# A fourth tile for raw weights, loads one unit earlier, and two sums of the last gate and up columns made by accumulating DMAs: a float32 decoder block on one Trainium2 core

## The chip, the cores and the metric

One Trainium2 chip, of which the program uses one core. The metric is the device time of one execution in microseconds (us): the median of three runs, and beside it one execution that the hardware profiler recorded.

## What is computed

The reference is one decoder block in float32 on x of 512 tokens by 2048 channels. Cut to what matters here:

```python
h = modulate(rms_norm(x, g_mix), sh1, sc1)        # the mixing half: w_in, two attentions, w_out
...
h = modulate(rms_norm(x, g_ffn), sh2, sc2)        # the feed-forward half
a = causal_dwconv(h @ w_gate, conv_w, conv_b)     # w_gate: 2048 x 5632
y = (jax.nn.silu(a) * (h @ w_up)) @ w_down        # w_up: 2048 x 5632, w_down: 5632 x 2048
x = x + gt2 * y
return rms_norm(x, g_final)
```

The change concerns the way in which weights reach TensorE. Most of its lines are in helpers that every projection uses, and what it alters in the work of an engine other than the queues is in the feed-forward half: gate, up and down.

## The kernel before, in words

**Units.** Every projection is cut into units, each a block of a weight matrix of about 128 x 1024 to 128 x 1792 numbers. A unit passes through a pipeline: SP loads the raw block from HBM into a tile of pool `wraw` (3 tiles); ScalarE (ACT) copies it into a rounded high part `wh` (L226 or L230), VectorE (DVE) subtracts that from the raw block to make the low part `wl` (L227 or L231), both in pool `wsp` (3 tiles each); TensorE (PE) then makes three products per pair of factors (high by high, high by low, low by high: L334 to L336 in `mm3`).

**Seven products.** The gate, up, down, w_out and most of the w_in gate columns use a Strassen-Winograd scheme: seven products of half blocks in place of eight, each of them three matmuls. A unit holds two sets of seven, so it is 2 x 7 x 3 = 42 matmuls with 256 moving columns. The weight side needs seven blocks b0 to b6, of which four are raw quarters of the weight block and three are sums. They are made in two ways:

- kind "seven" (gate, up, w_out, w_in gates; `US`): SP loads the four quarters with two DMAs (L183); DVE makes the first two sums in one instruction (L212) and the two that follow from them in two more (L213, L214).
- kind "right" (down; `UR`): SP loads one quarter twice into the places of the first two sums (L191), then the other three (L192, L193); GpSimd (POOL) issues two accumulating DMAs that add a second quarter to each from HBM (L195), after the loads have landed. DVE makes only L213 and L214.

**The look-ahead.** `ahead()` runs before each unit's products are emitted, and keeps three units converted. When it converts unit n it first emits the loads up to unit n + 2 (with L195, where the unit has it), then the copy and subtraction of unit n, then the sums of unit n + 1. With three raw tiles the load of unit n + 2 writes into the tile of unit n - 1, so SP waits there until L227 of unit n - 1 has ended; what stands behind it on SP waits too. Every engine executes in the order in which the program emits; nothing is reordered.

**The order of the feed-forward half.** 44 columns of gate and up with four units each (`proj_seven`, 22 pairs), with `combine` (L448 to L455), the convolution (L1437 to L1444) and the gating (L1459) of earlier columns in between; the gated result goes to HBM in tiles `g` (L1463). Then the down projection in three chunks of 8, 8 and 6 steps: for each chunk, columns of 512 outputs (4, 4 and 3 of them), each of 8, 8 or 6 units, 82 units in all. The left factors of a chunk are made from `g` (loads L1600, sums L1610 to L1613, parts L1627 to L1633) during the last gate/up column, the last column of the chunk before or the first column of the chunk. At the end of a column ACT copies the eight PSUM banks out (`leave`, L467), DVE combines (L473 to L479), and the result is stored by SP (L1672, first chunk) or added to the stored one by POOL (L1674, second chunk). The last 512 outputs of the last chunk are six plain units (L201, L230, L231).

All other intermediate data lives in `slots`, a pool of 65 tiles of 128 x 512. `first_ada`, in the first 200 us, loads the columns of w_ada ahead into such slots (L292).

Of the kernel before, what the change touches and what calls it, by code (L numbers as in the profile page):

```python
# [37 lines left out]
NSLOT = 65  # L38
# [52 lines left out]
OF2 = 1  # L91

# [12 lines left out]
def block_kernel(ctx, tc, x, c, w_ada, b_ada, g_mix, w_in, w_o_sb, w_o_dsa, w_out, rel_bias,  # L105
# [12 lines left out]
    wraw = pool("wraw", 3)  # L118
# [19 lines left out]
    units, raws, summed_, parts, at = [], [], [], [], [0]  # L138
# [5 lines left out]
    def US(w, k0, c0, fn):  # L144
        steps.append(((w, k0, 4, c0, 256, "seven"), fn))
        units.append(steps[-1][0])

    def UR(w, k0, c0, fn):
        steps.append(((w, k0, 2, c0, 512, "right"), fn))
        units.append(steps[-1][0])  # L150
# [21 lines left out]
    def seven_blocks(r, kind):  # L172

        q = 2 if kind == "seven" else 1
        return r.rearrange("p (q b c) -> p q b c", q=q, b=8)

    def load(spec):
        w, k0, nk, c0, nn, kind = spec
        raw = wraw.tile([128, 2048], F32, tag="raw", name="raw")
        if kind == "seven":  # L180
            for i in range(2):
                k = 128 * (k0 + 2 * i)
                nc.sync.dma_start(raw[:, 1024 * i + 512:1024 * (i + 1)].rearrange("p (k n) -> p k n", n=nn),  # L183
                                  w[k:k + 256, c0:c0 + nn].rearrange("(k p) n -> p k n", p=128))
            return raw
        if kind == "right":

            b = seven_blocks(raw, kind)[:, 0]
            wb = w[128 * k0:128 * (k0 + 2), c0:c0 + nn].rearrange("(k p) (u c) -> p k u c", p=128, u=2)
            for u in range(2):  # L190
                nc.sync.dma_start(b[:, 2 + u], wb[:, 1, 1])  # L191
            nc.sync.dma_start(b[:, 4:6], wb[:, 0])  # L192
            nc.sync.dma_start(b[:, 6], wb[:, 1, 0])  # L193
            for u in range(2):
                nc.gpsimd.dma_start(b[:, 2 + u], wb[:, u, 1 - u], accum_op=OP.add)  # L195
            return raw
# [7 lines left out]

    def sums_of(r, spec):

        kind = spec[5]
        if kind not in ("seven", "right"):
            return
        b = seven_blocks(r, kind)  # L210
        if kind == "seven":
            nc.vector.tensor_add(b[:, :, 2:4], b[:, :, 5:7], b[:, :, 7:8].to_broadcast([128, 2, 2, 128]))  # L212
# [3 lines left out]
    def convert(r, spec):  # L216
# [4 lines left out]
        if kind in ("seven", "right"):  # L221
            b = seven_blocks(r, kind)
# [1256 lines left out]
    for i in range(2):  # L1479
        proj_seven([ffn[-2 + i][0]], h2)  # L1480
# [303 lines left out]
```

## Time and profile before

| what | value |
|---|---|
| median of three runs | 3045.23 us (3038.62 to 3046.95) |
| the profiled execution, its own time | 3040.32 us |
| its span | 3038.6 us |
| mean granted TensorE clock | 0.972 |
| HBM read / written | 453.10 MB / 51.92 MB |

The span is the time from the first to the last recorded instruction; 1.7 us lie around it. The rows of the trace are read as follows. In a table of windows, each row gives a stretch of the span, then the busy time of each engine with the number of its instructions, the granted TensorE clock, the mean busy share of the 16 DMA engines and what they moved. In a list of waits, "A line <- B line: total, times, longest" says how long an engine stood still before an instruction, and whose end let it go. In a timeline, a row has start, duration, engine, line, what is written and read, and in brackets the idle time before it with what ended that.

### The profile page before, as it was taken

The page shows a single profiled execution, that of the slowest core. Times are in us where ns is not written, and L with a number is a line of the kernel's source. Part 1 is how long each engine was busy: PE and PEld are TensorE (multiplying, and loading weights), DVE is VectorE, ACT ScalarE, POOL GpSimd, SP SyncE. Part 2 cuts the span into 40 slices and gives each one's busy share as a digit, 9 for nine tenths or more (in the row PEclk, how much of TensorE's full clock was granted, in tenths as well). Part 3 has the DMA queues.
Part 4 walks back from the last instruction along what each step waited for, and adds up shares of the span by engine and source line. Part 5 has one row for each costly group of instructions (what it writes and reads, how often), then busy time and mean ns, then how long its engine had stood idle before and what let it go on. Part 6 is the DMA issues. An engine that isn't in the chain of part 4 may idle for free.

```text
span 3038.6 us, 52325 instructions
## 1 busy us (share of the span) xinstructions
PE 2890.5 (95%) x20287; PEld 2717.8 (89%) x20287; DVE 2496.0 (82%) x3677; ACT 1272.7 (42%) x1580; POOL 345.7 (11%) x372
## 2 busy tenths in 40 slices
PE   6899999999999999999988999999999999989887
PEld 5778889888888999888988999999999989989886
DVE  6877888888888887469989989988998997686778
ACT  4345433333344444224454444444444444353544
POOL 0000222201122000000122000000000013324330
PEclk8989999999999999999989999999999999989998
DMA  9664247777763445543452333333333357778996
GB/s 290 214 188 136 74 143 234 238 254 251 249 205 103 131 132 174 181 145 105 160 174 84 125 117 120 119 119 112 119 119 119 125 165 194 200 194 193 218 224 211
DMA packets 428520, 505.87 MB, mean 166 GB/s; under 512 B 34159, under 2 KB 328687, under 8 KB 428271
## 3 DMA queue, kind: packets, MB, share of 16 engines
q1 hardware_dynamic: 395439, 464.24, 48.2%
q0 software_dynamic: 25920, 25.70, 5.6%
q10 hardware_dynamic: 6912, 12.59, 1.1%
q8 instruction: 158, 2.59, 0.4%
q14 instruction: 91, 0.75, 0.1%
HBM read 453.10 MB, written 51.92 MB: 166 GB/s over the span
## 4 chain that ended last, share of the span: by engine, by line
PE 65%; DVE 15%; DMA 7%; issue 4%; ACT 2%; SPq 1%; POOL 0%; ACTq 0%; DVEq 0%; POOLq 0%
PE ps L334 21%; PE ps L336 21%; PE ps L335 21%; DMA raw<-in_w_down_dram 5%; DVE wl L227 4%; ACT wh L226 1%; DVE raw L213 1%; PE ps L957 1%; DVE slot L417 1%; DVE raw L212 1%; DVE slot L1633 1%; DVE raw L214 1%; DVE wl L231 0%; DMA slot<-x 0%; SPq L191 0%
## 5 line engine op out<-in xcount | busy, mean ns | idle before, releaser
L335 PE MATMUL ps<-slot,wh 128*128 128x256 f32 (+2 forms) x4624 | 1433.8, 310 | 18.8 <-DVE slot L412 16.4
L336 PE MATMUL ps<-slot,wl 128*128 128x256 f32 (+2 forms) x4624 | 1432.9, 310 | 10.4 <-DVE wl L227 10.4
L334 PE MATMUL ps<-slot,wh 128*128 128x256 f32 (+2 forms) x4624 | 1438.3, 311 | 4.1 <-ACT slot L411 2.4
L335 PEld LDWEIGHTS ps<-slot,wh 128*128 128x128 f32 (+1 forms) x4624 | 892.5, 193 | 63.4 <-DVE slot L412 18.0
L336 PEld LDWEIGHTS ps<-slot,wl 128*128 128x128 f32 (+1 forms) x4624 | 892.2, 193 | 57.1 <-DVE wl L227 12.6
L334 PEld LDWEIGHTS ps<-slot,wh 128*128 128x128 f32 (+1 forms) x4624 | 892.8, 193 | 50.8 <-ACT slot L751 4.5
L226 ACT CAST wh<-raw 128x1792 fp32r<-128x1792 f32 x338 | 571.2, 1695 | 716.5 <-DVE raw L214 404.8
L227 DVE TENSOR_TENSOR wl<-raw,wh 128x1792 fp32r<-128x1792 f32 x338 | 682.5, 2019 | 119.2 <-ACT wh L226 115.4
L334 PE MATMUL ps<-wh,slot 128*128 128x256 f32 (+1 forms) x1708 | 503.1, 295 | 35.0 <-ACT slot L467 29.8
L335 PE MATMUL ps<-wl,slot 128*128 128x256 f32 (+1 forms) x1708 | 500.8, 293 | 18.8 <-DVE wl L227 18.3
L336 PE MATMUL ps<-wh,slot 128*128 128x256 f32 (+1 forms) x1708 | 499.4, 292 | 4.8 <-DVE slot L514 4.8
L334 PEld LDWEIGHTS ps<-wh,slot 128*128 128x128 f32 x1708 | 338.0, 198 | 41.7 <-ACT slot L467 31.9
L335 PEld LDWEIGHTS ps<-wl,slot 128*128 128x128 f32 x1708 | 338.1, 198 | 24.0 <-DVE wl L227 21.0
L336 PEld LDWEIGHTS ps<-wh,slot 128*128 128x128 f32 x1708 | 338.0, 198 | 8.8 <-DVE slot L514 6.8
L231 DVE TENSOR_TENSOR wl<-raw,wh 128x1024 fp32r<-128x1024 f32 (+3 forms) x178 | 209.9, 1181 | 82.7 <-ACT wh L230 78.4
L195 POOL DMA_DIRECT2D raw<-in_w_down_dram x164 | 145.4, 1012 | 1154.5 <-DVE slot L1459 845.7
L230 ACT CAST wh<-raw 128x1024 fp32r<-128x1024 f32 (+3 forms) x178 | 177.5, 998 | 236.6 <-PE ps L335 172.5
L212 DVE TENSOR_TENSOR raw<-raw 128x512 f32<-128x512 f32 x256 | 178.2, 696 | 28.7 <-DMA raw<-in_w_up_dram 10.9
L213 DVE TENSOR_TENSOR raw<-raw 128x256 f32<-128x256 f32 x338 | 151.6, 449 | 56.2 <-DMA raw<-in_w_down_dram 47.3
L545 DVE SCALAR_TENSOR_TENSOR slot<-slot,c_act 128x512 f32<-128x512 f32 x240 | 192.0, 800 | 6.8
L214 DVE TENSOR_TENSOR raw<-raw 128x256 f32<-128x256 f32 x338 | 155.7, 461 | 11.6
L1266 POOL TENSOR_TENSOR mask<-mask,slot 128x512 f32<-128x512 f32 x13 | 19.0, 1458 | 553.5 <-ACT slot L1265 553.0
(224 smaller groups left out, 2241.6 us busy)
## 6 DMA issues: line engine op xcount, KB each, us to landing
slot<-in_w_ada_dram SPq DMA_DIRECT2D x368, 256.0 KB, 4.9
raw<-in_w_in_dram SPq DMA_DIRECT2D x118, 512.0 KB, 5.1
raw<-in_w_gate_dram SPq DMA_DIRECT2D x176, 256.0 KB, 3.1
raw<-in_w_up_dram SPq DMA_DIRECT2D x176, 256.0 KB, 3.1
raw<-in_w_down_dram SPq DMA_DIRECT2D x246, 128.0 KB, 4.2
raw<-in_w_in_dram SPq DMA_DIRECT2D x114, 256.0 KB, 2.9
raw<-in_w_down_dram SPq DMA_DIRECT2D x82, 256.0 KB, 4.7
raw<-in_w_down_dram POOLq DMA_DIRECT2D x164, 128.0 KB, 4.6
```

The source lines that it names most:

```text
L195: nc.gpsimd.dma_start(b[:, 2 + u], wb[:, u, 1 - u], accum_op=OP.add)
L212: nc.vector.tensor_add(b[:, :, 2:4], b[:, :, 5:7], b[:, :, 7:8].to_broadcast([128, 2, 2, 128]))
L213: nc.vector.tensor_add(b[:, :, 1], b[:, :, 3], b[:, :, 5])
L214: nc.vector.tensor_add(b[:, :, 0], b[:, :, 4], b[:, :, 1])
L226: nc.scalar.copy(hf, f)
L227: nc.vector.tensor_sub(l.rearrange("p (q f) -> p q f", q=n), f, hf.bitcast(F32))
L230: nc.scalar.copy(h, r)
L231: (nc.gpsimd if kind else nc.vector).tensor_sub(l, r, h.bitcast(F32))
L334: nc.tensor.matmul(o, lhsT=sh, rhs=mh, start=start, stop=False, skip_group_check=skip)
L335: nc.tensor.matmul(o, lhsT=sh, rhs=ml, start=False, stop=False, skip_group_check=skip)
L336: nc.tensor.matmul(o, lhsT=sl, rhs=mh, start=False, stop=stop, skip_group_check=skip)
L545: nc.vector.scalar_tensor_tensor(acc, raw[n], s, acc, op0=OP.mult, op1=OP.add)
```

## The change

- Pool `wraw` has 4 tiles, of 128 x 1792 in place of 128 x 2048; `slots` has 63 tiles in place of 65, and `first_ada` looks ahead `20 - len(hT)` in place of `22 - len(hT)` (never over 10).
- The seven blocks lie without a gap (7 blocks, not 8). In kind "seven" the quarter that is added to two others is loaded into the place of b0, so its load is three DMAs in place of two.
- `ahead()`, before the conversion of unit n, emits the loads up to unit n + 3, then the accumulating loads up to unit n + 2 (now a function of its own, `loaded_sums`), then the sums up to unit n + 1, and then the conversion of unit n.
- Kind "right" becomes "seven by dma", which also takes units of 4 x 128 rows by 256 columns. The gate and up columns from the 15th of the 19 pairs of the middle loop on, and those of the last two pairs, use it: 5 + 2 = 7 pairs by the code (the change's own words say eight), 14 columns, 56 units. Each loads five quarters with four DMAs on SP and adds two with two accumulating DMAs on POOL; DVE's L212 falls away there.

The diff, cut to its core:

```diff
-NSLOT = 65
+NSLOT = 63
+BY_DMA = 14
-    wraw = pool("wraw", 3)
+    wraw = pool("wraw", 4)
...
     def load(spec):
         w, k0, nk, c0, nn, kind = spec
-        raw = wraw.tile([128, 2048], F32, tag="raw", name="raw")
...
+        raw = wraw.tile([128, 1792], F32, tag="raw", name="raw")
+        if is_seven(spec):
+            b, wb = seven_blocks(raw, spec)
+            for u in (2, 3) if kind == "seven by dma" else (0,):
+                nc.sync.dma_start(b[:, :, u], wb[:, :, 1, 1])
+            nc.sync.dma_start(b[:, :, 4:6], wb[:, :, 0])
+            nc.sync.dma_start(b[:, :, 6], wb[:, :, 1, 0])
             return raw
...
+    def loaded_sums(r, spec):
+
+        if spec[5] == "seven by dma":
+            b, wb = seven_blocks(r, spec)
+            for u in range(2):
+                nc.gpsimd.dma_start(b[:, :, 2 + u], wb[:, :, u, 1 - u], accum_op=OP.add)
...
         while len(parts) < min(at[0] + 3, len(units)):
             n = len(parts)
-            loads(n + 3)
-            sums(n + 1 if units[n][5] == "right" else n + 2)
+            loads(n + 4)
+            while len(added_) < min(n + 3, len(units)):
+                loaded_sums(raws[len(added_)], units[len(added_)])
+                added_.append(True)
+            sums(n + 2)
             parts.append(convert(raws[n], units[n]))
             raws[n] = None
-            sums(n + 2)
...
-            first_load(n + min(AHEAD, 22 - len(hT)))
+            first_load(n + min(AHEAD, 20 - len(hT)))
...
     for n, (g, u) in enumerate(ffn[1:-2]):
-        proj_seven([g], h2)
-        proj_seven([u], h2)
+        proj_seven([g], h2, by_dma=n >= BY_DMA)
+        proj_seven([u], h2, by_dma=n >= BY_DMA)
...
-        proj_seven([ffn[-2 + i][0]], h2)
+        proj_seven([ffn[-2 + i][0]], h2, by_dma=True)
...
-    proj_seven([ffn[-2][1]], h2, left_start)
-    proj_seven([ffn[-1][1]], h2, h2_end)
+    proj_seven([ffn[-2][1]], h2, left_start, by_dma=True)
+    proj_seven([ffn[-1][1]], h2, h2_end, by_dma=True)
```

The order of the instructions on PE and ACT is the same in both kernels. It differs on DVE, SP and POOL. Lines of the changed kernel are shifted: its L190 to L192 are the loads that were L191 to L193 (and L183), its L207 the accumulating load L195, its L216 and L217 the sums L213 and L214, its L225 and L226 the copy and the subtraction that were L226 and L227, its L1464 and L1601 the former L1463 and L1600.

DVE in the second column of the first down chunk, before. The numbers behind `raw`, `wl` and `wh` name the tile of one unit; a subtraction reads the raw tile and writes `wl`:

```order
L227 TENSOR_TENSOR wl_27019<-raw_26855,wh_27018 128x1792
L213 TENSOR_TENSOR raw_26937<-raw_26937 128x256
L214 TENSOR_TENSOR raw_26937<-raw_26937 128x256
L227 TENSOR_TENSOR wl_27074<-raw_26937,wh_27073 128x1792
L213 TENSOR_TENSOR raw_27011<-raw_27011 128x256
L214 TENSOR_TENSOR raw_27011<-raw_27011 128x256
```

The same place of the changed kernel:

```order
L216 TENSOR_TENSOR raw_27228<-raw_27228 128x256
L217 TENSOR_TENSOR raw_27228<-raw_27228 128x256
L226 TENSOR_TENSOR wl_27394<-raw_27173,wh_27393 128x1792
L216 TENSOR_TENSOR raw_27310<-raw_27310 128x256
L217 TENSOR_TENSOR raw_27310<-raw_27310 128x256
L226 TENSOR_TENSOR wl_27449<-raw_27228,wh_27448 128x1792
```

Before, the two sums of a unit stand directly ahead of the subtraction of the same unit (26937, 26937). In the changed kernel the subtraction of the unit before stands between them (27228, then 27173, then 27310, then 27228): the sums went one place forward past one subtraction.

SP where gate and up end and down begins, before. `in_w_up` and `in_w_down` are the weights, `g3` and `g40` are tiles of the gated result in HBM, read back and stored:

```order
L1600 DMA slot_25908<-g3_17143 128x512
L183 DMA raw_25911<-in_w_up_dram 128x2x256 x2
L183 DMA raw_25963<-in_w_up_dram 128x2x256 x2
L191 DMA raw_26032<-in_w_down_dram 128x256 x2
L192 DMA raw_26032<-in_w_down_dram 128x512
L193 DMA raw_26032<-in_w_down_dram 128x256
L1463 DMA g40_26092<-slot_25554 128x512
```

The same place of the changed kernel:

```order
L1601 DMA slot_26276<-g3_17248 128x512
L190 DMA raw_26279<-in_w_up_dram 128x2x128 x2
L191 DMA raw_26279<-in_w_up_dram 128x2x256
L192 DMA raw_26279<-in_w_up_dram 128x2x128
L190 DMA raw_26334<-in_w_down_dram 128x256 x2
L191 DMA raw_26334<-in_w_down_dram 128x512
L192 DMA raw_26334<-in_w_down_dram 128x256
L190 DMA raw_26406<-in_w_down_dram 128x256 x2
L191 DMA raw_26406<-in_w_down_dram 128x512
L192 DMA raw_26406<-in_w_down_dram 128x256
L1464 DMA g40_26465<-slot_25904 128x512
```

Between the same two DMAs, SP loaded the last two up units and the first down unit before, and loads the last up unit and the first two down units now: all loads stand one unit earlier among SP's other DMAs. An up unit is four DMAs now (L190 twice, L191, L192) where it was two (L183 twice). On POOL, 56 pairs of accumulating loads for gate and up now stand ahead of those for down, where it had nothing to do before; the order of its other work is the same.

More of the change, by code (lines that the diff above doesn't have):

```diff
@@ L137, in block_kernel @@
     steps = []
-    units, raws, summed_, parts, at = [], [], [], [], [0]
+    units, raws, added_, summed_, parts, at = [], [], [], [], [], [0]
     def U(w, k0, nk, c0, nn, fn, early=False):
@@ L142, in U, with US @@
         units.append(steps[-1][0])
[L144 to L145 removed]
+    def US(w, k0, c0, fn, by_dma=False):
+        steps.append(((w, k0, 4, c0, 256, "seven by dma" if by_dma else "seven"), fn))
         units.append(steps[-1][0])
     def UR(w, k0, c0, fn):
[L149 removed]
+        steps.append(((w, k0, 2, c0, 512, "seven by dma"), fn))
         units.append(steps[-1][0])
@@ L169, in drain, with seven_blocks, is_seven @@
             advance(q)
-    def seven_blocks(r, kind):
-        q = 2 if kind == "seven" else 1
-        return r.rearrange("p (q b c) -> p q b c", q=q, b=8)
+    def seven_blocks(r, spec):
+        w, k0, nk, c0, nn, kind = spec
+        q = nk // 2
+        return (r.rearrange("p (q b c) -> p q b c", q=q, b=7),
+                w[128 * k0:128 * (k0 + nk), c0:c0 + nn].rearrange("(q k p) (u c) -> p q k u c", q=q, p=128, u=2))
+    def is_seven(spec):
+        return isinstance(spec[5], str)
     def load(spec):
         w, k0, nk, c0, nn, kind = spec
-        raw = wraw.tile([128, 2048], F32, tag="raw", name="raw")
[L180 to L195, printed above, removed]
+        raw = wraw.tile([128, 1792], F32, tag="raw", name="raw")
[5 more added lines that the diff above has]
+            nc.sync.dma_start(b[:, :, 6], wb[:, :, 1, 0])
             return raw
@@ L203, in load @@
         return r
+    def loaded_sums(r, spec):
[3 more added lines that the diff above has]
+                nc.gpsimd.dma_start(b[:, :, 2 + u], wb[:, :, u, 1 - u], accum_op=OP.add)
     def sums_of(r, spec):
-        kind = spec[5]
-        if kind not in ("seven", "right"):
+        if not is_seven(spec):
             return
-        b = seven_blocks(r, kind)
-        if kind == "seven":
-            nc.vector.tensor_add(b[:, :, 2:4], b[:, :, 5:7], b[:, :, 7:8].to_broadcast([128, 2, 2, 128]))
+        b, _ = seven_blocks(r, spec)
+        if spec[5] == "seven":
+            nc.vector.tensor_add(b[:, :, 2:4], b[:, :, 5:7], b[:, :, 0:1].to_broadcast([128, 2, 2, 128]))
         nc.vector.tensor_add(b[:, :, 1], b[:, :, 3], b[:, :, 5])
@@ L220, in convert @@
         l = wsp.tile([128, 1792], F32R, tag="wl", name="wl")
-        if kind in ("seven", "right"):
-            b = seven_blocks(r, kind)
-            n, c = b.shape[1], b.shape[3]
-            f = b[:, :, 0:7].rearrange("p q b c -> p q (b c)")
-            hf = h.rearrange("p (q f) -> p q f", q=n)
-            nc.scalar.copy(hf, f)
-            nc.vector.tensor_sub(l.rearrange("p (q f) -> p q f", q=n), f, hf.bitcast(F32))
-            return tuple(v.rearrange("p (q b c) -> p q b c", q=n, b=7) for v in (h, l))
+        if is_seven(spec):
+            nc.scalar.copy(h, r)
+            nc.vector.tensor_sub(l, r, h.bitcast(F32))
+            return tuple(v.rearrange("p (q b c) -> p q b c", q=spec[2] // 2, b=7) for v in (h, l))
         h, l = h[:, 0:r.shape[1]], l[:, 0:r.shape[1]]
@@ L479, in combine_right, with proj_seven @@
         nc.vector.tensor_sub(y1[:, b], y1[:, b], v[:, a])
-    def proj_seven(ws, factors, before=None, k1=KT, plain=None, k2=None):
+    def proj_seven(ws, factors, before=None, k1=KT, plain=None, k2=None, by_dma=False):
         st = [None] * len(ws)
```

2 lines of the change are left out of this document (1 added, 1 removed).

## The prediction

> **What bounds the kernel now.** The page comes first: which engine is nearest to full.
>
> ```profile
> span 3038.6 us, 52325 instructions
> PE 2890.5 (95%) x20287; PEld 2717.8 (89%) x20287; DVE 2496.0 (82%) x3677; ACT 1272.7 (42%) x1580; POOL 345.7 (11%) x372
> ```
>
> PE is busy 95% of the span, so what can be won is PE's idle and slow time, and the question is where that lies. The table of windows answers it, by PE's count of matmuls: first a stretch of gate and up, then the down projection, cut where the left factors of a chunk are made (first, third and fifth) and where they are not.
>
> ```profile
> core 0: us, PE busy (x) PEld busy (x) DVE busy (x) ACT busy (x) POOL busy (x), PEclk, DMA share, GB/s
> 2200.00:2400.00 200.00, 200.00 (x1669) 200.00 (x1668) 180.87 (x239) 84.33 (x70) 0.00 (x0) 1.00 0.38 119
> 2475.00:2550.00 75.00, 64.08 (x480) 62.57 (x479) 68.87 (x115) 39.45 (x51) 20.25 (x24) 0.91 0.78 200
> 2550.00:2675.00 125.00, 119.94 (x976) 118.72 (x975) 80.55 (x119) 48.72 (x48) 38.51 (x44) 0.99 0.82 207
> 2675.00:2725.00 50.00, 37.62 (x255) 36.80 (x254) 45.01 (x82) 26.01 (x37) 12.22 (x14) 0.83 0.72 182
> 2725.00:2850.00 125.00, 118.43 (x951) 117.25 (x950) 78.23 (x112) 47.52 (x47) 49.85 (x57) 0.97 0.88 198
> 2850.00:2925.00 75.00, 60.20 (x454) 58.83 (x453) 61.00 (x106) 38.69 (x53) 23.80 (x28) 0.93 0.90 223
> ```
>
> In gate and up PE never stops, at full clock: 1669 matmuls in 200 us, 8.345 per us, so a unit of 42 takes 5.03 us. Nothing done there by other engines can make it shorter. In down the counts fall short of that pace. Per stretch, (8.345 x length - count) / 8.345 gives 17.5, 8.0, 19.4, 11.0 and 20.6 us: 57.5 us in the three bursts of left factors and 19.0 us in the two steady stretches, 76.5 us together. That is all the change can reach for there. DVE is 92%, 90% and 81% busy in the bursts, only about 63% in the steady stretches.
>
> Next the waits from 2400 us on: first PE's own, then what PE's releasers wait for, then SP's.
>
> ```profile
> PE ps L334 <- ACT slot L467: 29.8, 9, 5.2
> PE ps L335 <- DVE wl L227: 18.3, 12, 3.6
> ...
> ACT wh L226 <- DVE raw L214: 215.0, 60, 9.0
> POOL raw L195 <- DMA raw<-in_w_down_dram: 170.7, 54, 8.3
> DVE raw L213 <- DMA raw<-in_w_down_dram: 47.3, 28, 5.3
> ...
> SPq L191 <- DVE raw L213: 161.8, 42, 6.7
> SPq L191 <- DVE wl L227: 82.4, 26, 4.7
> SPq L1672 <- DVE slot L476: 34.3, 7, 9.5
> ```
>
> PE waits for low parts (L227) and, at the end of a column, for ACT's copies out of PSUM (L467). ACT stands behind a copy that waits for sums (L214), which wait for accumulating DMAs, which wait for loads, which wait on SP for a free raw tile: a ring. One turn of it, from the timelines of SP, POOL, DVE, ACT, DVE and SP:
>
> ```profile
> 2612.45 0.86 SPq L191 DMA_DIRECT2D raw<-in_w_down_dram  x2
> 2616.87 1.75 POOL L195 DMA_DIRECT2D raw<-in_w_down_dram  x2 [3.87 <-DMA raw<-in_w_down_dram]
> 2623.32 0.43 DVE L213 TENSOR_TENSOR raw<-raw 128x256 f32<-128x256 f32 x1 [1.51 <-DMA raw<-in_w_down_dram]
> 2624.36 1.69 ACT L226 CAST wh<-raw 128x1792 fp32r<-128x1792 f32 x1 [4.61 <-DVE raw L214]
> 2626.09 2.03 DVE L227 TENSOR_TENSOR wl<-raw,wh 128x1792 fp32r<-128x1792 f32 x1 [1.88 <-ACT wh L226]
> 2628.14 0.81 SPq L191 DMA_DIRECT2D raw<-in_w_down_dram  x2
> ```
>
> Each arrow follows its predecessor's end at once. From a load to the load that reuses its tile: 2628.14 - 2612.45 = 15.69 us, 10.87 of them from the load to L213. Three tiles make that 5.23 us per unit, more than PE's 5.03. So in down the ring, not PE, sets the pace, and what a column's end costs is never made up.
>
> **The fourth tile and the order.** The load of unit n + 3 still starts when L227 of unit n - 1 ends, since the tile is that of n - 1. Its sums now stand ahead of L227 of unit n + 2, whose copy was made a unit earlier. So the ring no longer passes through ACT: load to L213 10.87, the sums 0.89 (2623.32 to where L214 ends, 0.46 + 0.43, as long again for L214 as for L213), L227 2.03, together 13.8 us for three units. That is 1.9 less, the copy and its hops (2624.21 to 2626.09), and 4.6 us per unit, below PE's 5.03. It is not a whole unit of slack: the added tile is spent on the earlier sums.
>
> The edit adds a wait: L213 of unit n + 1 now stands ahead of L227 of unit n. Where an accumulation is late, L227, the combining and the left factors are queued behind L213 on DVE, and PE (`wl`), SP (tile) and, at chunk 1, POOL's additions wait for them. It costs nothing while the ring is below 5.03.
>
> *Steady stretches.* They hold (976 + 951) / 42 = 46 units. 0.20 us each is the ring's excess: 9.2 us, taken back whole. The other 9.8 us are column ends, where SP stands in L1672 behind the combining (34.3 us) and the next loads behind it; a ring with 0.4 us to spare per unit makes up some 3 us per column of 8. I take half, 5 us. Bounds: 9 and 19; taken 14.
>
> *Bursts.* They hold 1189 / 42 = 28 units, 9.4 turns. If the ring bound them, 9.4 x 1.9 = 18 us would go; if DVE bound them all through, nothing. DVE's idle time is 6.1 + 5.0 + 14.0 us of 200, so mostly DVE binds. Bounds 0 and 18; taken 6, the third nearest to DVE.
>
> **Sums by DMA in the last seven pairs.** Removed: 56 times L212. While PE is never idle this is worth nothing. It counts where DVE becomes late for PE, at the end of gate and up:
>
> ```profile
> L212 DVE TENSOR_TENSOR raw<-raw x7: 680/684/694, 2440.9 to 2475.9; 128x512 f32<-128x512 f32 x7
> ...
> 2475.00:2525.00 50.00, 42.85 (x327) 41.54 (x326) 49.32 (x86) 26.37 (x35) 13.23 (x16) 0.93 0.84 220
> ...
> 2499.11 0.58 PE L334 MATMUL ps<-wh,slot 128*128 128x256 f32 x1 [4.20 <-DVE slot L449]
> ```
>
> DVE is full from 2475 us, and PE waits 4.20 us for `combine`. The seven L212 ahead of that are 7 x 0.684 = 4.8 us of a full DVE; bounds 0 and 4.8; taken 4.8, since PE stands directly behind DVE there.
>
> Added: per unit two more DMAs on SP (4 in place of 2, 0.43 each, 1.7 us of 5.03), two issues on POOL, idle there, and 896 KB in place of 512. No trace shows a unit of this kind in gate or up, so its DMA time is bounded by packets. The queues' rows, in turn for 600 to 800, 2050 to 2250, 2550 to 2675 and 2725 to 2850 us, and the landing of the loads of down:
>
> ```profile
> q1 hardware_dynamic: 34862, 49.93, 75.2%
> ...
> q1 hardware_dynamic: 23008, 23.24, 37.2%
> ...
> q0 software_dynamic: 6336, 5.77, 31.0%
> ...
> q0 software_dynamic: 7903, 8.77, 45.4%
> ...
> raw<-in_w_down_dram SPq DMA_DIRECT2D x246, 128.0 KB, 4.2
> raw<-in_w_down_dram POOLq DMA_DIRECT2D x164, 128.0 KB, 4.6
> L195 POOL DMA_DIRECT2D raw<-in_w_down_dram x164: 853/865/1534, 2474.1 to 2969.0; - x164
> ```
>
> Share x 16 x window / packets is a packet's time: 69.0 ns at 1432 B and 51.7 at 1010 for plain loads, 114.9 at 1110 and 97.9 at 911 for accumulating ones. On these lines a 512-byte packet is 31 ns plain, 64 accumulating (estimates). A unit is 768 plain packets of 512 B, 256 of 1 KB (52 ns) and 512 accumulating of 512 B: 70.2 engine-us, on 16 engines 4.4 us of 5.03. The stores of `g` (two DMAs of 128 packets of 2 KB, 94 ns each on the same line, per eight units) add 0.2. So the cover, PE's 5.03 us, holds with a tenth to spare; a down unit by the same lines is 3.7 us, 4.5 with POOL's additions. Should an accumulating packet of 512 B take as long as one of 1 KB (107 ns), it is 6.0 us per unit and the cover is gone: (6.0 - 5.03) x 56 = 54 us. Taken: 0; ends 0 and 54. The Trainium skill, "DMA: Bandwidth & Descriptors", Specifications, puts the smallest size at line rate at 512 B. By that rule (an estimate from bytes alone) the unit would be 3.8 us; the lines above ask a little more, and no run here has an accumulating packet that small.
>
> **The rest.** A load of kind "seven" is three DMAs in place of two (0.43 us more of SP's 5.03, beside PE at 100%). Two slots fewer, and two fewer columns of w_ada ahead, can hold SP up where a slot is not free. In down and at the start:
>
> ```profile
> SPq L1600 <- PE ps L336: 2.3, 5, 1.0
> ...
> PE ps L678 <- DVE slot L698: 29.8, 7, 11.2
> ```
>
> SP waits 2.3 us for slots that PE frees; PE's waits at the start are for DVE's arithmetic, not its loads. Bounds 0 and 3 us, taken 1. The conversion reads 1792 numbers without a gap in place of twice 896: the same count, 0.
>
> Sum: 14 + 6 + 4.8 - 1 = 24 us. Against the profiled execution, 3040.32 - 24 = 3016; the median of the three runs lies 4.9 us above that execution, so 3021.
>
> **The rivals.**
>
> 1. *The ring is not the bound; DVE and the ends of columns are.* Then PE would wait for ACT and DVE as now, and only L212 counts: 3045.2 - 5 = 3040. For it: DVE's 92% and 90% in the bursts, and L467 as PE's longest wait. Against: DVE at 63% in steady stretches that still lose 19 us, and a ring of 15.69 us with no gap in it. The Trainium skill gives a rule that leads here, in "DMA: Bandwidth & Descriptors", Anatomy of one DMA: a DMA issued by GpSimd takes 2.0 us plus its bytes over 436 GB/s. By that, 128 KB would land in 2.3 us (an estimate) and the ring would be 13.4 us, 4.5 per unit, before any change. The trace has 4.6 us, and decides. Chance 0.17.
> 2. *Slower: accumulating packets of 512 B choke gate and up.* Its place is the 56 units before down, its price 54 us, less the 24 won: 3045.2 + 30 = 3075. It decides from 78 ns per packet on (what 5.03 - 0.2 leaves beside 37.4 engine-us of plain packets, over 512). For it: accumulating queues are the dearest by the byte here, and L213's stall would now hold L227 back. Against: both queues' rows grow with size. Chance 0.11.
> 3. *More: the bursts are bound by the ring as well.* 19 + 18 + DVE's 4.8 and some lead into each burst, 45 to 50 us: 2997. For it: DVE idles 14 us in the last burst. Against: DMA's share is already 0.90 there. Chance 0.08.
>
> **How the numbers follow.** The forecast, 3021, has 0.64. Its own bounds are 9 + 0 + 0 - 3 = 6 and 19 + 18 + 4.8 = 42 us won, 3039 to 3003. The range 3000 to 3046 holds it and the first rival with the spread of runs, and leaves out the second and third, 0.19. A measurement of this kernel can tell about 0.3% (9 us) from no change. Faster by more: 0.64 + 0.08 = 0.72; within: 0.17; slower: 0.11.
>
> **What would show it.** In the profile after: 5.03 to 5.1 us per unit between column ends (1030 to 1043 matmuls in 125 us of steady down); L227's wait for ACT nearly gone, L213's wait for DMA kept; ACT's wait for L216/L217 well below 215 us, and PE's for L467 about halved; gate and up at 1669 per 200 us to their end, with a DMA share near 0.9 in the last 280 us. It is wrong if PE has gaps in gate and up, if steady down stays at 5.4 us, or if DVE's stall at the sums grows by as much as ACT's wait shrinks.

## The result, and the profile after

| | before | after |
|---|---|---|
| median of four runs, side by side | 3043.32 us | 3014.10 us (3010.35 to 3018.54) |
| ratio of the times, 95% interval | | 0.9905 (0.9885 to 0.9926) |
| the profiled execution: time, span | 3040.32, 3038.6 us | 3015.27, 3013.6 us |
| mean granted TensorE clock | 0.972 | 0.976 |

The changed kernel is 29 us faster. Medians here and below leave out executions of several thousand us, of which experiments 1 and 7 had one each. Its line numbers are shifted: L190 to L192 load a seven-block tile, L207 accumulates, L215 to L217 are the sums (L212 to L214 before), L225 the copy and L226 the low part. PE's matmuls are L335 to L337, ACT's copies out of PSUM L468, `combine` starts at L450, and the accumulating stores of sums are L1675. The page after, first the engines:

```profile
span 3013.6 us, 53120 instructions
PE 2879.1 (96%) x20287; PEld 2706.0 (90%) x20287; DVE 2449.6 (81%) x3621; ACT 1276.8 (42%) x1580; POOL 480.6 (16%) x484
```

PE is 11.4 us less busy and the span 25.0 us shorter: what went is PE's idle and slow time. The table of windows after, with the last of gate and up first and then down, cut again at the bursts:

```profile
core 0: us, PE busy (x) PEld busy (x) DVE busy (x) ACT busy (x) POOL busy (x), PEclk, DMA share, GB/s
2200.00:2400.00 200.00, 198.40 (x1647) 197.60 (x1646) 150.21 (x196) 82.31 (x69) 94.75 (x78) 1.00 0.90 190
2475.00:2550.00 75.00, 63.15 (x481) 61.91 (x480) 68.43 (x113) 40.13 (x50) 20.99 (x24) 0.91 0.83 214
2550.00:2650.00 100.00, 100.00 (x836) 100.00 (x835) 68.48 (x100) 41.92 (x40) 34.83 (x40) 1.00 0.88 222
2650.00:2725.00 75.00, 66.29 (x516) 64.93 (x515) 68.88 (x119) 42.83 (x57) 22.55 (x26) 0.95 0.83 211
2725.00:2850.00 125.00, 116.84 (x947) 115.25 (x945) 80.69 (x121) 49.45 (x50) 48.45 (x57) 0.99 0.91 203
```

Three things stand here. The steady stretch of chunk 0 has 836 matmuls in 100 us, PE's full pace. That of chunk 1 still has only 947 in 125 us (951 before). And the end of gate and up, where PE never stopped before, has 1647 in 200 us in place of 1669, with DMA's share up from 0.38 to 0.90.

The waits after, from 2400 us on:

```profile
DVE raw L216 <- DMA raw<-in_w_down_dram: 90.7, 37, 5.9
ACT wh L225 <- DVE raw L217: 87.2, 37, 7.8
...
PE ps L336 <- DVE wl L226: 25.7, 18, 3.6
POOL sum L1675 <- DVE slot L478: 22.6, 5, 12.5
POOL sum L1675 <- ACT slot L468: 20.3, 3, 8.4
...
PE ps L335 <- ACT slot L468: 7.6, 7, 2.3
```

PE's wait for ACT at a column's end is 7.6 us (29.8 before), ACT's for the sums 87.2 (215.0). In exchange DVE's stall at L216 grew from 47.3 to 90.7 us, and PE's wait for low parts of down from 18.3 to 25.7.

To see where 25 us come from, the two traces must be laid on each other by program points, not by the clock. One such point is SP's store of `g` of one pair in the middle of gate and up, here before and after:

```profile
1886.91 0.94 SPq L1463 DMA_DIRECT2D g<-slot  x2
```

```profile
1880.45 0.94 SPq L1464 DMA_DIRECT2D g<-slot  x2
```

Others are PE's first matmul at the second norm, before and after, and (after alone; 2499.11 us before) the matmul that waits for the last `combine` of gate and up, with a stall ahead of it that is new:

```profile
1557.76 1.87 PE L1345 MATMUL ps<-ones,slot 128*128 128x1 f32 x8 [4.93 <-ACT slot L1283]
```

```profile
1553.64 0.60 PE L1346 MATMUL ps<-ones,slot 128*128 128x1 f32 x4 [0.79 <-ACT slot L1284]
...
2479.87 0.58 PE L337 MATMUL ps<-slot,wl 128*128 128x256 f32 x1 [4.73 <-DVE wl L226]
...
2499.48 0.58 PE L335 MATMUL ps<-wh,slot 128*128 128x256 f32 x1 [3.92 <-DVE slot L450]
```

The changed kernel is 6.5 us ahead in the middle of gate and up (1880.45 against 1886.91), of which 4.1 us are PE's shorter wait at the norm, and 0.4 us behind at their end. From there I count PE's matmuls, 336 to a column of chunks 0 and 1 (40.3 us at 8.345 per us):

| stretch | before, us | after, us | won |
|---|---|---|---|
| chunk 0, first column (burst) | 49.8 | 44.2 | 5.6 |
| chunk 0, columns 2 to 4 | 137.1 | 123.8 | 13.4 |
| chunk 1, first column (burst) | 53.6 | 51.4 | 2.1 |
| chunk 1, columns 2 to 4 | 138.4 | 135.9 | 2.5 |
| chunk 2 and the rest | 160.6 | 158.8 | 1.8 |

Down won 25.4 us. (The fourth column of a chunk also makes left factors for the next chunk, so this table does not cut where the prediction's windows did; that cut comes in the part on why.) The lead of 6.5 us before it was lost again in the 56 units that are summed by DMA. So three questions were open: what in the edit won in down, where the early lead is from, and why the tail of gate and up costs 7 us.

### The profile page after: what moved, and what is told of

It is laid out like the page before. It is cut to its first block, busy times and chain, and to the rows that moved or that the text cites. A ratio compares the mean times of both kernels' runs of the same rounds, so it can differ in the third digit from the quotient of the medians.

```text
span 3013.6 us, 53120 instructions
## 1 busy us (share of the span) xinstructions
PE 2879.1 (96%) x20287; PEld 2706.0 (90%) x20287; DVE 2449.6 (81%) x3621; ACT 1276.8 (42%) x1580; POOL 480.6 (16%) x484
## 4 chain that ended last, share of the span: by engine, by line
PE 66%; DVE 17%; DMA 10%; issue 3%; ACT 2%; SPq 1%; POOL 1%; ACTq 0%; DVEq 0%; POOLq 0%
PE ps L335 21%; PE ps L336 21%; PE ps L337 21%; DVE wl L226 6%; DMA raw<-in_w_down_dram 6%; DMA raw<-in_w_up_dram 1%; DVE raw L216 1%; DVE slot L418 1%; PE ps L679 1%; DVE slot L1634 1%; PE ps L958 1%; ACT wh L225 1%; DVE raw L215 1%; SPq L190 1%; DMA slot<-in_w_ada_dram 1%
## 5 line engine op out<-in xcount | busy, mean ns | idle before, releaser
L336 PE MATMUL ps<-slot,wh 128*128 128x256 f32 (+2 forms) x4624 | 1433.2, 310 | 20.4 <-DVE slot L413 17.7
L337 PE MATMUL ps<-slot,wl 128*128 128x256 f32 (+2 forms) x4624 | 1432.1, 310 | 16.7 <-DVE wl L226 16.6
L335 PE MATMUL ps<-slot,wh 128*128 128x256 f32 (+2 forms) x4624 | 1438.0, 311 | 2.9 <-ACT slot L723 1.4
L337 PEld LDWEIGHTS ps<-slot,wl 128*128 128x128 f32 (+1 forms) x4624 | 891.8, 193 | 63.8 <-DVE wl L226 19.7
L335 PEld LDWEIGHTS ps<-slot,wh 128*128 128x128 f32 (+1 forms) x4624 | 892.2, 193 | 49.8 <-ACT slot L752 4.5
L225 ACT CAST wh<-raw 128x1792 fp32r<-128x1792 f32 x338 | 570.6, 1694 | 622.0 <-DVE raw L217 207.4
L226 DVE TENSOR_TENSOR wl<-raw,wh 128x1792 fp32r<-128x1792 f32 x338 | 682.2, 2019 | 68.0 <-ACT wh L225 67.6
L336 PE MATMUL ps<-wl,slot 128*128 128x256 f32 (+1 forms) x1708 | 497.1, 291 | 25.9 <-DVE wl L226 25.7
L335 PE MATMUL ps<-wh,slot 128*128 128x256 f32 (+1 forms) x1708 | 497.4, 291 | 11.9 <-ACT slot L468 7.6
L337 PE MATMUL ps<-wh,slot 128*128 128x256 f32 (+1 forms) x1708 | 495.4, 290 | 4.3 <-DVE slot L515 4.3
L335 PEld LDWEIGHTS ps<-wh,slot 128*128 128x128 f32 x1708 | 333.6, 195 | 17.2 <-ACT slot L468 9.0
L337 PEld LDWEIGHTS ps<-wh,slot 128*128 128x128 f32 x1708 | 333.5, 195 | 8.1 <-DVE slot L515 5.9
L216 DVE TENSOR_TENSOR raw<-raw 128x256 f32<-128x256 f32 x338 | 150.4, 445 | 148.2 <-DMA raw<-in_w_down_dram 90.7
L207 POOL DMA_DIRECT2D raw<-in_w_down_dram x164 | 145.7, 1042 | 266.2 <-DMA raw<-in_w_down_dram 134.7
L207 POOL DMA_DIRECT2D raw<-in_w_gate_dram x56 | 68.8, 1471 | 641.7 <-DVE wl L226 558.2
L217 DVE TENSOR_TENSOR raw<-raw 128x256 f32<-128x256 f32 x338 | 154.7, 458 | 11.6
L215 DVE TENSOR_TENSOR raw<-raw 128x512 f32<-128x512 f32 x200 | 139.2, 696 | 0.0
```

What stands on the lines that cost most here:

```text
L207: nc.gpsimd.dma_start(b[:, :, 2 + u], wb[:, :, u, 1 - u], accum_op=OP.add)
L215: nc.vector.tensor_add(b[:, :, 2:4], b[:, :, 5:7], b[:, :, 0:1].to_broadcast([128, 2, 2, 128]))
L216: nc.vector.tensor_add(b[:, :, 1], b[:, :, 3], b[:, :, 5])
L217: nc.vector.tensor_add(b[:, :, 0], b[:, :, 4], b[:, :, 1])
L225: nc.scalar.copy(h, r)
L226: nc.vector.tensor_sub(l, r, h.bitcast(F32))
```

## The experiments

Each kernel carries a ratio to the kernel before, which ran beside it. Differences between two kernels below are differences of these ratios, on 3042 us. Stretches are read from each kernel's profiled execution.

**1. The tail on DVE again.** All gate and up units of the changed kernel summed on DVE:

```diff
-        proj_seven([g], h2, by_dma=n >= BY_DMA)
-        proj_seven([u], h2, by_dma=n >= BY_DMA)
+        proj_seven([g], h2)
+        proj_seven([u], h2)
...
```

The last two pairs lose `by_dma=True` as well.

> The changed kernel with all gate and up units summed on DVE again (four tiles, the new order and 63 slots kept). Theory 1, the tail by DMA costs time: in the changed kernel the lead of 6.4 us that stands until pair 14 is gone when gate and up end (PE's waits for L226 there, 7 us, 4.73 of them one stall while SP stands 6.8 us in the read of g). Without the tail by DMA the lead is kept: about 6 us faster than the changed kernel's 3014, so 3006 to 3010, PE without gaps to 2470. Theory 2, as the prediction had it: taking the first sums from a full DVE is worth 4.8 us, so without it 3017 to 3020. Theory 3, the two slots fewer are the whole loss: the stall is the same here, 3014 within 2.

Measured 3004.9 us, ratio 0.9872 (0.9857 to 0.9888): theory 1. By the ratios the tail by DMA costs 10 us, uncertain by some 8, where the prediction had it win 4.8. Gate and up end at 2492.87 us, the lead kept, 6.6 us ahead of the changed kernel: so much is the tail's. Another 5.6 us of the two profiled executions lie in columns 2 to 4 of chunk 1 (130.3 and 135.9 us), where both kernels execute the same instructions. The kernel of experiment 6, with more units by DMA, takes 130.9 us there, so that part can't be put down to the tail.

**2. Sums from DMA in the last two columns only.**

```diff
-        proj_seven([g], h2, by_dma=n >= BY_DMA)
-        proj_seven([u], h2, by_dma=n >= BY_DMA)
-        proj_seven([ffn[-2 + i][0]], h2, by_dma=True)
+        proj_seven([g], h2)
+        proj_seven([u], h2)
+        proj_seven([ffn[-2 + i][0]], h2)
```

> The changed kernel with sums from DMA only in the last two columns of up (8 of 56 units), where DVE also makes left factors. Theory 1a, the chain of load, accumulation and sums is too long for the lead it has, in every unit: the small waits before 2460 us (1.9 us) go, the 4.73 us stall of the last column stays: 3011 to 3013. Theory 1b, it is only late where DMA has been busy for 250 us: the stall goes too and DVE's relief of 8 x 0.68 = 5 us shows: 3003 to 3007. Theory 2, DVE's relief in all seven pairs counts: 3017 to 3019.

Measured 3010.7 us, 0.9889 (0.9875 to 0.9903): nearest to theory 1a. Eight units bring the stall, and DVE's relief does not show. PE's row in that kernel:

```profile
2477.65 0.58 PE L337 MATMUL ps<-slot,wl 128*128 128x256 f32 x1 [5.46 <-DVE wl L226]
```

**3. Four tiles, the old order of the sums** (tail by DMA kept):

```diff
-            sums(n + 2)
+            sums(n + 1 if units[n][5] == "seven by dma" else n + 2)
             parts.append(convert(raws[n], units[n]))
             raws[n] = None
+            sums(n + 2)
```

> The changed kernel with the sums in the order of before (those of a unit summed by DMA stand behind the low part of the unit ahead of it); four tiles, 63 slots and the tail by DMA kept. Theory 1, the ring is what paced down: with four tiles and ACT in it a turn is 15.69 us for four units, 3.9 us per unit, as far below PE's 5.03 as the changed kernel's 4.6, so steady stretches at 8.3 matmuls per us and 3006 to 3016. Theory 2, the copy's wait for the sums at a column's end is what cost, and the order took it away: PE's wait for ACT at L468 is back at 25 to 30 us from 2400 us on, and the time is 3030 to 3040.

Measured 3032.9 us, 0.9963 (0.9949 to 0.9977). The time fits theory 2, its reason does not: PE's wait for ACT at the columns' ends is 17.6 us from 2400 us on, where theory 2 asked for 25 to 30. Two windows of that kernel, the last of gate and up, then steady down:

```profile
2200.00:2400.00 200.00, 193.63 (x1595) 191.64 (x1594) 141.92 (x183) 75.73 (x63) 91.05 (x75) 1.00 0.88 186
2575.00:2675.00 100.00, 100.00 (x835) 100.00 (x835) 66.95 (x93) 40.99 (x40) 35.14 (x41) 1.00 0.91 226
```

Steady down runs at full pace (835 in 100 us), as the ring with four tiles asks. The loss lies in gate and up (1595 matmuls in 200 us): there the old order sums a unit so late that PE waits in every pair, and from 2192 us of before to the end of gate and up it loses 22 us against before. This kernel could not tell what the order is worth in down; experiment 5 can.

**4. Three tiles, the new order.**

```diff
-    wraw = pool("wraw", 4)
+    wraw = pool("wraw", 3)
...
-            loads(n + 4)
+            loads(n + 3)
```

> The changed kernel with three raw tiles and loads one unit less ahead; the new order of the sums, 63 slots and the tail by DMA kept. Theory 1, the ring: from a load to the low part that its sums stand ahead of is 13.8 us in down, now for two units, so 6.9 us per unit against 5.03 over 82 units, and about 6.3 in the 56 units of the tail: 3014 + 150 + 70, between 3170 and 3260; the lead of 6.4 us before 1650 us is gone too. Theory 2, the new order alone takes ACT's wait away and the tile matters little: 3010 to 3045.

Measured 3186.4 us, 1.0469 (1.0451 to 1.0487): theory 1. Two windows, gate and up by DMA and steady down, and PE's matmul at the norm:

```profile
2300.00:2400.00 100.00, 85.57 (x664) 83.86 (x663) 61.00 (x80) 31.44 (x28) 37.07 (x31) 0.95 0.72 155
2625.00:2775.00 150.00, 122.92 (x926) 120.38 (x925) 77.17 (x112) 49.47 (x50) 38.57 (x45) 0.93 0.70 168
```

```profile
1563.01 0.37 PE L1346 MATMUL ps<-ones,slot 128*128 128x1 f32 x1 [6.01 <-ACT slot L1284]
```

A unit of 42 matmuls takes 42 x 150 / 926 = 6.80 us in steady down (6.9 expected) and 42 x 100 / 664 = 6.33 us in gate and up (6.3 expected). A ring whose length was read from one turn of the trace before gives the pace of a kernel with another number of units in it to 2%. And with three tiles the wait at the norm is back (6.01 us): the early lead is the fourth tile's, with the load one unit earlier that it allows. What it does there stands in DVE's timeline of before:

```profile
1550.67 0.69 DVE L212 TENSOR_TENSOR raw<-raw 128x512 f32<-128x512 f32 x1 [3.33 <-DMA raw<-in_w_gate_dram]
```

The last `combine` of w_out stood on DVE behind the sums of the next gate unit, whose load came late. With a tile more the load is there, and in the changed kernel DVE has no such wait.

**5. The old order, tail on DVE:** experiments 1 and 3 together.

> The changed kernel with the order of the sums of before and with gate and up summed on DVE: of the change, only the fourth tile, the loads one unit ahead, the tile's new form and the 63 slots are left. In the two four-tile kernels so far the time from the last combining of gate and up to the end is 514.1 us with the new order and 512.8 with the old one, 539.5 before. Theory 1, the fourth tile alone is the gain in down and the new order adds nothing there: 510 to 514 us for that stretch and 3003 to 3010 in all, as with the new order and the same tail (3005.5). Theory 2, the new order is worth something in the bursts, where DVE is full: 3011 to 3020, with PE's waits for L226 in 2650 to 2725 us above the changed kernel's 7.2.

Measured 3010.9 us, 0.9901 (0.9887 to 0.9914), 0.0029 or 9 us above the same kernel with the new order, at the lower edge of theory 2. PE's waits in down, with the old order (lines shifted by one) and with the new:

```profile
PE ps L336 <- ACT slot L469: 20.1, 8, 4.1
...
PE ps L337 <- DVE wl L226: 14.0, 13, 3.6
```

```profile
PE ps L336 <- DVE wl L226: 25.9, 18, 3.9
...
PE ps L335 <- ACT slot L468: 4.5, 5, 1.3
```

The new order takes the copy that waits for sums out of ACT's way, 15.6 us at the columns' ends, and gives 11.9 back as later low parts. Theory 2's reason fell all the same: from 2650 to 2725 us L226's waits are 5.0 us, where it asked for more than 7.2. In the two profiled executions down, to PE's last matmul, takes 503.5 us with the old order and 496.0 with the new. The order is worth 9 us by the ratios (uncertain by 6) and 7.5 in down; the waits named here account for 3.7 of them, the rest stays open.

**6. All pairs but the first by DMA** (`BY_DMA = 0`).

> The changed kernel with 21 pairs of gate and up summed by DMA in place of seven (all but the first). Theory 1, the longer chain makes the low part late now and then in every pair: the five pairs before the last two lost 2 to 4 us, so 14 more pairs cost 6 to 14: 3020 to 3028, with small waits of PE for L226 all through gate and up. Theory 2, the loss lies in the change-over to down alone, where SP stands in the read of g: 3012 to 3017. Theory 3, the DMA engines choke on packets of 512 bytes once it lasts: 3060 and more, with DMA's share at 1.0.

Measured 3017.6 us, 0.9921 (0.9908 to 0.9935), 5 us over the changed kernel, which the intervals don't settle; theory 3 fell. PE's waits from 1650 to 2470 us, which take in all its units by DMA but the last eight, and the stall after them:

```profile
PE ps L337 <- DVE wl L226: 6.6, 12, 1.6
```

```profile
2487.22 0.58 PE L337 MATMUL ps<-slot,wl 128*128 128x256 f32 x1 [5.96 <-DVE wl L226]
```

PE's idle time in these waits is 6.6 us, but what it loses is more: matched matmul by matmul with before, its lead shrinks from 8.3 us at 1712 us of before to a lag of 2.1 at 2450, by 10.4 us over the 160 units, and the stall at the end takes another 5.9. In the changed kernel the 48 units before the last eight cost 2.5 us the same way. So within gate and up theory 1 holds, small waits all through, 8 us more for 112 units more (it said 6 to 14); the total hides them, as chunk 1 came out 5 us shorter in this execution.

**7. The reads of `g` one unit later.** In the changed kernel SP stands in the first four reads of `g` for the left factors, with the loads of up's last units behind them. SP's rows of before and of after, and the unit on DVE that this makes late:

```profile
2457.89 3.15 SPq L1600 DMA_DIRECT2D slot<-g  x4
```

```profile
2456.97 8.56 SPq L1601 DMA_DIRECT2D slot<-g  x4
```

```profile
2477.00 0.43 DVE L216 TENSOR_TENSOR raw<-raw 128x256 f32<-128x256 f32 x1 [5.27 <-DMA raw<-in_w_up_dram]
```

```diff
-LS = 8
+LS = 12
```

> The changed kernel with the first reads of g for the left factors one unit later (unit 4 of the last but one column of up in place of unit 3). Theory 1, the stall at the end of gate and up comes from SP standing in that read for a slot (8.56 us for four reads in the changed kernel, 3.15 before) with the loads of two units of up behind it: the slot comes free at the column's end, so a read one unit later waits about 3 us; PE's 4.73 us shrink to 2 or less, and 3008 to 3012. Theory 2, the loads are late there for the length of the chain itself, or the later reads make the left factors late: 3013 to 3020, the waits only change their name.

Measured 3006.5 us, 0.9886 (0.987 to 0.9901): theory 1, a little better than it asked. SP's four reads and PE's row in that kernel:

```profile
2459.35 3.70 SPq L1601 DMA_DIRECT2D slot<-g  x4
```

```profile
2478.68 0.39 PE L337 MATMUL ps<-slot,wl 128*128 128x256 f32 x1 [0.98 <-DVE wl L226]
...
2491.96 0.58 PE L335 MATMUL ps<-wh,slot 128*128 128x256 f32 x1 [3.93 <-DVE slot L450]
```

The stall shrinks to 0.98 us, and gate and up end at 2491.96 us, as with the tail on DVE (2492.87). In the changed kernel one of the four reads stood 6.8 us for a slot that PE frees at the column's end.

**8. The slots alone.** The kernel before with 63 slots and two columns of w_ada less ahead:

> The kernel before with 63 slots and two fewer columns of w_ada ahead, nothing else. Theory 1, the slots cost next to nothing by themselves: 3042 to 3048 where the kernel before has 3044. Theory 2, they are the reason for the changed kernel's stall at the end of gate and up (SP 6.8 us in the read of g, PE 4.73 us): SP stands there for 5 us or more here too, and the time is 3049 or more.

Measured 3054.1 us, 1.0042 (1.0028 to 1.0056): two slots cost 13 us (9 to 17), theory 2. SP's first four reads of `g` take 11.17 us there, 3.15 before. At the second norm this kernel is 0.5 us later than before (1558.27 against 1557.76 us), so the shorter look-ahead of w_ada at the start is not what costs. PE's stall at the end of gate and up, and its waits in down:

```profile
2478.26 0.39 PE L336 MATMUL ps<-slot,wl 128*128 128x256 f32 x1 [3.53 <-DVE wl L227]
```

```profile
PE ps L334 <- ACT slot L467: 31.9, 10, 4.7
...
PE ps L335 <- DVE wl L227: 24.4, 17, 3.6
```

Gate and up end 7.4 us later than before (2506.56 against 2499.11 us). In down the two waits are 56.3 us together, 48.1 before (29.8 + 18.3); no single column or wait carries that difference.

**9. One slot less in the changed kernel** (62, and 19 for 20 in `first_ada`).

> The changed kernel with one slot less (62) and one column of w_ada less ahead. Theory 1, slots are scarce at the change-over and in down, as two fewer cost the kernel before 13 us (ratio 1.0042): 5 to 10 us slower than the changed kernel, 3019 to 3025. Theory 2, the price is a threshold or the fourth tile covers it: 3012 to 3017.

Measured 3020.7 us, 0.9923 (0.9911 to 0.9936): 5 us more by the ratios, whose intervals overlap. PE's stall at the same place grew from 4.73 to 6.34 us. That points to theory 1, without settling it: the profiled execution, 3014.0 us, is the fastest of the five, and no slower than the changed kernel's.

**10. POOL's head of line in chunk 1.** Steady columns of chunk 1 had won almost nothing. Around a column's end of the changed kernel, POOL and DVE:

```profile
2754.58 3.52 POOL L207 DMA_DIRECT2D raw<-in_w_down_dram  x4 [5.82 <-DVE raw L217]
2766.47 0.87 POOL L1675 DMA_DIRECT2D sum<-slot  x1 [8.37 <-ACT slot L468]
2767.60 0.87 POOL L1675 DMA_DIRECT2D sum<-slot  x1 [0.26 <-issue]
2768.20 2.06 POOL L207 DMA_DIRECT2D raw<-in_w_down_dram  x2
```

```profile
2761.66 0.42 DVE L216 TENSOR_TENSOR raw<-raw 128x256 f32<-128x256 f32 x1 [5.95 <-DMA raw<-in_w_down_dram]
...
2762.46 2.02 DVE L226 TENSOR_TENSOR wl<-raw,wh 128x1792 fp32r<-128x1792 f32 x1
2764.39 0.42 DVE L474 TENSOR_TENSOR slot<-slot 128x256 f32<-128x256 f32 x1
```

Read them together. POOL stands 8.37 us in L1675, the store of a column's sums, which needs the combining at L474 to L480. On DVE that is queued behind L216, which waits 5.95 us for an accumulation. Meanwhile the accumulations of later units are queued on POOL behind L1675. Each queue's stall lengthens the other's. With the tail on DVE, the stores are issued one unit after their combining:

```diff
                 combine_right(*e)
...
+                if i == 1:
+                    yield
                 for t, y in enumerate(e[0:2], 2 * p):
...
                 del e
-                yield
+                if i == 0:
+                    yield
```

> The kernel with the tail by DVE (3005.5), and in chunk 1 each pair of accumulating stores of sums is issued one unit after its combining. Theory 1, POOL's head of line: in the changed kernel POOL stands 8.4 us in L1675 for the combining, which stands on DVE behind L216, which waits for accumulations queued behind L1675; that is why the three steady columns of chunk 1 gained nothing (959 matmuls in 125 us, where chunk 0 runs at 8.44 per us). With the stores a unit later POOL does not stand there, and 4 to 7 of the 10 us come back: 2998 to 3002. Theory 2, DMA traffic is the limit there (share 0.85 to 1.0): 3004 to 3007, PE's waits for L226 in chunk 1 unchanged.

(The 959 and 8.44 of that text are sums of 25 us windows, which count a matmul at an edge twice; one window gives 947 and 8.36.) Measured 2995.8 us, 0.9851 (0.9838 to 0.9865), better than theory 1 asked. The same 125 us of the kernel without and with the edit:

```profile
2710.00:2835.00 125.00, 118.79 (x976) 117.23 (x975) 84.86 (x128) 51.92 (x51) 51.15 (x58) 1.00 0.93 210
```

```profile
2710.00:2835.00 125.00, 122.66 (x1019) 122.07 (x1017) 89.02 (x134) 54.87 (x56) 51.38 (x59) 1.00 0.95 220
```

43 matmuls more, 5 us, at a DMA share that is not lower but higher: traffic was not the limit. In these 125 us POOL's idle time ahead of the stores falls from 27.1 to 4.9 us. Columns 2 to 4 of chunk 1 take 125.0 to 127.0 us in the three kernels with this edit and 130.3 us or more in every kernel without it.

**11 and 12. Both delays together,** with the tail on DVE and with the tail by DMA.

> The fastest kernel so far (tail by DVE, accumulating stores of chunk 1 one unit later: 2995.8, ratio 0.9851) with the reads of g one unit later as well. Theory 1, SP's stand in the read (10.4 us there) costs PE 2 to 3 us at the change-over: 2991 to 2995, ratio 0.984. Theory 2, without the tail by DMA the loads of the fourth tile already cover it: 2995 to 2999, or slower by some us, since the first left factors come later.

> The changed kernel, tail by DMA kept, with the reads of g one unit later and the accumulating stores of chunk 1 one unit after their combining: against the same kernel with the tail by DVE (2995.5, ratio 0.9846) it leaves the tail as the one difference, with SP's stand gone. Theory 1, DVE's relief at the end of gate and up is worth the 4.8 us of the prediction once the stall is away: 2989 to 2992, ratio 0.983. Theory 2, it is worth nothing, as gate and up end at 2492 us in both kernels looked at so far: 2994 to 2998. Theory 3, the longer chain still costs some us by itself: 2999 to 3003, ratio 0.986 or more.

Measured 2995.5 us, 0.9846 (0.9832 to 0.9859), and 2995.9 us, 0.9854 (0.9838 to 0.9871). Theory 2 both times: with SP out of the way, the tail by DMA is worth nothing and costs nothing that can be measured. They and number 10 are the fastest kernels, 0.5% below the changed one; which of the three is ahead can't be told.

## Why the prediction was right, and where not

Put side by side, the kernels split the change. From before: two slots fewer, +13 us (1.0042); with that, the fourth tile and the loads ahead, -43 (0.9901); the new order, -9 (0.9872); the tail by DMA, +10 (0.9905). Each difference of two ratios is uncertain by 0.2 to 0.25% (6 to 8 us). The parts hold for this order of adding them: without the fourth tile the new order would not win at all (experiment 4, with three tiles, is 143 us slower than before). The sum, -29, has the prediction's sign and nearly its size of -24, but not its terms.

- *The ring.* Its length was read right, the way in which it costs was not. It said 5.23 us per unit before and 4.6 after, under PE's 5.03. The three-tile kernel gave 6.80 us where the same turn said 6.9, and chunk 0 after runs at PE's full pace. But "0.20 us each is the ring's excess" did not show in the units: chunk 0 before was mostly at full pace too, except where a column ends. The two windows are of before; the second holds the end of a column, and 25 us at full pace are 209 matmuls:

```profile
2600.00:2625.00 25.00, 25.00 (x210) 25.00 (x210) 12.18 (x14) 7.40 (x5) 8.77 (x10) 1.00 0.82 195
2625.00:2650.00 25.00, 21.66 (x167) 21.39 (x167) 16.46 (x27) 9.71 (x13) 5.75 (x7) 0.93 0.80 223
```

  From a unit's first matmul to that of the next unit, 35 of the 42 units that are not the last of their column (columns 2 to 4 of chunks 0 and 1, before) take 5.03 to 5.08 us. The six last ones take 5.6 to 12.8, and hold 28.9 of the 33.9 us that these columns lose. With the fourth tile and the old order (experiment 5) the six columns lose 23.5 us, with the new order too (experiment 1) 11.4. So the ring came due at the columns' ends, where ACT's copies out of PSUM stand behind a copy that waits for sums. That the units converted ahead cover it in between fits these numbers, but no run shows it by itself.

  The prediction put the gain on the order, with "the added tile is spent on the earlier sums". The runs put 43 us on the tile, counted from the kernel with two slots fewer (30 from before), and 9 on the order: with the tile alone the ring is 15.69 / 4 = 3.9 us, an estimate from the same turn. Of its signs, ACT's wait for the sums shrank (215.0 to 87.2 us), and DVE's stall behind DMA was not just kept but grew by 43.4 us, less than ACT's wait shrank. One sign of being wrong came true: PE has gaps in gate and up.
- *Steady stretches,* 14 us (9 to 19). Sized too high. Followed matmul by matmul from the prediction's own windows, those of 2550 to 2675 us take 118.8 us after, and those of 2725 to 2850 take 126.7: 6.3 won and 1.7 lost, 4.6 together. In the six kernels with the new order and the stores of chunk 1 as they were, it is 4.6 to 9.6. (The 13.4 + 2.5 of columns 2 to 4 are more since a fourth column reaches into the next burst.) What held chunk 1 up was named, "at chunk 1, POOL's additions", but given no price: it is the 8.37 us of L1675, and it cost 5 us of chunk 1 (experiment 10).
- *Bursts,* 6 us (0 to 18). Sized too low, and for a wrong reason. The same way they won 5.8 (from 2499 us on) + 7.7 + 6.2 = 19.7 us, and 17.7 to 21.9 in the six kernels. The step that failed is "mostly DVE binds": in these three stretches of before PE waited 17.4 us for ACT's copies at a column's end and 13.3 for low parts from DVE; after, 1.7 and 16.5. With the tile and the old order 12.9 us of the wait for ACT are left, so it is the order that removed most of it. The prediction priced column ends in the steady stretches alone.
- *L212 at the end of gate and up,* 4.8 us (0 to 4.8). Wrong in sign. The step that failed is "PE stands directly behind DVE there". The gap before `combine` is 3.92 us with the tail by DMA and 3.92 with the tail on DVE (4.20 before): the seven L212 are not in it. They lie from 2440.9 to 2475.9 us, before the stretch in which DVE is full: in the trace before, DVE was busy 20.7 us of the 25 up to 2450 and 22.8 of the 25 up to 2475. And the sums that are left now wait for data (5.27 us at L216), not for DVE. The pair 11 and 12 shows the relief by itself: nothing that can be measured.
- *The tail's DMA,* 0 us (0 to 54). The packet prices held. The queues of the changed kernel from 2200 to 2470 us, plain and accumulating:

```profile
q1 hardware_dynamic: 57829, 37.68, 47.9%
q0 software_dynamic: 27961, 13.48, 40.9%
```

  0.409 x 16 x 270 / 27961 = 63.2 ns per accumulating packet, 64 estimated; 35.8 ns per plain one of mixed size, where the estimates mix to 36.3. DMA's share of 0.90 over 200 us and 1647 / 42 units is 4.6 us a unit, 4.4 + 0.2 estimated. The rule of the Trainium skill, "DMA: Bandwidth & Descriptors", Specifications (line rate from 512 B on), made it an estimated 3.8; the trace sides with the lines. Throughput was covered, as the prediction said. Lead was not: a load, then an accumulation, then a sum is a chain, and a few small waits and one stall of 4.73 us came through.
- *Two slots,* 1 us (0 to 3). This step failed far outside its bounds: 13 us alone. It read "SP waits 2.3 us for slots that PE frees" as the price with fewer slots, but that was the price with enough. With two fewer, the reads that took SP 3.15 us took it 11.17 (experiment 8) and 8.56 in the changed kernel. The fourth tile hid most of it where DVE summed (SP's and PE's rows of that kernel follow: 1.99 us of PE's time for 11.93 us of SP's), and the longer chain by DMA did not.

```profile
2450.85 11.93 SPq L1601 DMA_DIRECT2D slot<-g  x4
```

```profile
2479.60 0.39 PE L337 MATMUL ps<-slot,wl 128*128 128x256 f32 x1 [1.99 <-DVE wl L226]
```

- *What it did not see.* 6.5 us, won before the middle of gate and up, from the same tile: a load that was late for a `combine` queued behind it. 4.1 us of them are PE's wait at the norm (4.93 and 0.79 us), the others follow in the next 110 us. Its list of places with slack counted gate and up, where PE is full, and left the change-over ahead of them out.

The rivals: the first (the ring is not the bound, DVE and the columns' ends are) was right that PE's loss stood at the columns' ends, and wrong that tile and order leave it there. The second (choke) fell with 63.2 ns, below its 78. The third (more in the bursts) fell by its time, 2997, though its 18 us for the bursts were nearer than the forecast's 6.

So the time was forecast well in part by luck, as misses cancelled: 9.4 us less than taken in the steady stretches, 13.7 more in the bursts, 6.5 unforeseen at the norm, and some 7 to 10 lost at the tail where 4.8 were to be won. What stays open is how the 13 us of two slots divide in down, where no single wait carries them.

## What to carry to other kernels

Read one turn of a buffer ring from the timelines, with every queue it passes through, and divide by the units in it: that gave the pace of a kernel with one tile less within 2%. Then look where a small excess is paid: here not in each unit, but at the end of a column, where another queue stands behind the late one. A buffer that is taken from another pool has to be priced at the tightest place of that pool with fewer, not by the waits seen with enough. And a queue's head that waits for an engine which waits for that queue (POOL's store, DVE's sum) is worth more than the share of either: delaying one issue by a unit gave some 6 us at a DMA share of 0.93, which had looked like the limit.

## What the runs showed of the hardware

POOL's issue of an accumulating DMA of 128 KB takes longer when its pieces are smaller. The groups of L207 in the changed kernel:

```profile
L207 POOL DMA_DIRECT2D raw<-in_w_down_dram x164 | 145.7, 1042 | 266.2 <-DMA raw<-in_w_down_dram 134.7 <-DVE raw L217 40.6 <-DVE raw L216 22.0
L207 POOL DMA_DIRECT2D raw<-in_w_gate_dram x56 | 68.8, 1471 | 641.7 <-DVE wl L226 558.2 <-DMA raw<-in_w_gate_dram 56.5 <-DVE raw L217 12.0
```

1042 ns on average for 128 pieces of 1 KB (down), 1471 for 256 of 512 bytes (gate): 0.43 us for 128 pieces more, on an engine that has two such issues in each 5.03 us.
